# Moving the tiles of a projection kernel to other byte places, with a new order at its start and its end

## The chip, the cores and the metric

The kernel runs on one core of one Trainium2 chip. The metric is the device time of one execution in microseconds, as the median of several runs.

## What is computed

One layer of a streaming encoder, for a prompt of 4096 frames and a sample of 64 frames with a state, in float32:

```python
def mixer_layer(x, c, s_gla, s_hgrn, w_ada, b_ada, g_pre, w_in, w_alpha, b_alpha,
                g_on_gla, lb, g_on_hgrn, w_out, g_post):
    mod = jnp.einsum('bd,de->be', c, w_ada) + b_ada
    shift, scale, gate = jnp.split(mod, 3, axis=-1)
    h = rms_norm(x, g_pre) * (1 + scale[:, None]) + shift[:, None]
    p = jnp.einsum('btd,de->bte', h, w_in)               # 1024 x 3600
    q_a, k_a, v_a, z_a, a_lr, q_h, f_h, i_h, z_h = jnp.split(p, ...)
    log_alpha = log_sigmoid(a_lr @ w_alpha + b_alpha) / 16
    o_a, s_a = chunked_gla(q_a / 8, k_a, v_a, log_alpha, s_gla)      # 4 heads
    f = lb + (1.0 - lb) * sigmoid(f_h)
    o_h, s_h = chunked_gla(silu(q_h), 1.0 - f, i_h, log(f), s_hgrn)  # 4 heads
    o_a = rms_norm(o_a, g_on_gla) * silu(z_a)
    o_h = rms_norm(o_h, g_on_hgrn) * silu(z_h)
    o = jnp.concatenate([o_a, o_h], axis=-1) @ w_out     # 1024 x 1024
    return x + gate[:, None] * rms_norm(o, g_post), s_a, s_h
```

`chunked_gla` is a gated linear recurrence: the state decays by a gate in each frame and takes in key times value; the output is the query times the state.

## The kernel before

The prompt is cut into 16 groups of 256 frames; the sample's 64 frames ride along with one group in each part. The kernel has these parts, one after the other:

1. *Start* (`setup`, `first_group`). It loads x, the conditioning, the identity and eight rows of small vectors, normalises and turns the first group, computes the modulation from w_ada in eight steps of 128 features, and projects the first group in step with the arriving weights. Here the order is written out by hand.
2. *GLA part*, 16 groups (`proj_gla`). `proj_feat` (L594) computes q and k with features on the partitions, `tok_step` (L606) computes z and v with tokens on them. The recurrence of the group before (`attend`) is woven in at fixed stops.
3. *HGRN part*, 16 groups (`proj_hgrn`). f and q by `proj_feat`, i by `tok_step`; the recurrence is woven in.
4. *Last gates* (`z_tile`): z of the HGRN half by `tok_step`, tile by tile. The first stretch has the last recurrence beside it, the rest has TensorE's projections alone.
5. *Output projection* (`project`, product at L1391): 2 x 2 blocks by Strassen's scheme in Winograd's form, seven products of 12 matmuls for each group: A11 by B11, A12 by B21, S2 by T2, S3 by T3, S1 by T1, S4 by B22, A22 by T4; then norm, gate and store. The sample's rows are projected inside the last group.

Each float32 number is split into a rounded part and a rest (hi and lo), and a product has three terms: hi hi, hi lo, lo hi. A matmul has one operand that *stands* (loaded into the array, 128 columns) and one that *streams* (256 to 512 columns). The two differ between the helpers:

```python
for a, b in ((wh, hi), (wh, lo), (wl, hi)):                       # proj_feat, L593
    self.nc.tensor.matmul(ps[:, :T], a, b, ...)                   # weights stand, h streams
for i, (a, b) in enumerate(((hi, wh), (hi, wl), (lo, wh))):       # tok_step, L605
    self.nc.tensor.matmul(ps[:r, : c1 - c0], a, b, ...)           # h stands, weights stream
```

The tiles: `wa` (8 units of 4096 bytes per partition: weights of q and k, then f, then the last gates, then the blocks S1 to S4 and A22), `wv` (8 units of 4224 bytes: z, then q of HGRN, then output weights), `wb` (8 units of 4096 bytes: v, then i, then output weights), `wc` (12 units of output weights), `hh` (h split, 5 slots 5120 bytes apart), `hs` (pairs of the staging tile `wst`, used for A11 and A12). Pools are stacked from the left end of a partition's memory in the order const, small, w, then the recurrence or the output weights; x, h, e and the staging tiles are stacked from the right end. Inside a pool a tag's slots follow each other in the order of their first use.

The *place* of a tile in what follows is its byte address in its partition modulo 512. With the kernel's sizes the allocator gives:

| tile | place before |
|---|---|
| `wa`, `wb`, `wc` | 320 |
| `wv`, units in order | 320, 448, 64, 192, and again |
| `hh`, `hf`, `xt`, `e` | 224 |
| `hs` | 224 (A11) and 352 (A12) |
| `Xg`, `Qg`, `K`, `F`, `A`, `v`, `S` of the recurrence | 320 |
| `ident` | 128 |

The halves hi and lo, the steps of 128 columns and the features inside a tile are multiples of 256 or 512 bytes apart, except in `wv` while it holds z (528 columns wide), where the rest lies 64 and the second half of the columns 32 bytes further on.

TensorE executes in program order, and SP issues nearly all loads and stores in order. The planner keeps the order of most instructions on the other engines but may move some of them past each other, as in the end shown in the prediction.

Of the kernel before, what the change touches and what calls it, by code (L numbers as in the profile page):

```python
# [15 lines left out]
P = 128  # L16
D = 1024
# [11 lines left out]
class Kernel:  # L29
# [42 lines left out]
    def rstd(self, ms, n, table=False):  # L72
# [73 lines left out]
    def setup(self):  # L146
# [22 lines left out]
        nc.scalar.preload_act_table_set("natural_log_exp_and_others")  # L169
# [17 lines left out]
        with ExitStack() as s:  # L187
            one = self.pool(s, "setup")
            ap = self.pool(s, "ada", 3)

            rows = one.tile([52, P], F32, name="rows")
            v = lambda a: a.rearrange("(k p) -> k p", p=P)
            self.x_load(0, [0])
            nc.sync.dma_start(rows[0:8], v(t["c_prompt"][0]))
            nc.sync.dma_start(rows[8:16], v(t["c_sample"][0]))
            nc.sync.dma_start(self.ident, t["ident"])
            self.x_load(0, [1])
            few = [
                (rows[16:32], v(t["b_ada"][0, : 2 * D])),
                (rows[32:40], v(t["g_pre"][0])),  # L200
                (rows[40:42], v(t["b_alpha"][0])),
                (rows[42:50], t["hgrn_lb_logits"].rearrange("r (k p) -> (r k) p", p=P)),
                (rows[50:51], t["g_onorm_gla"]),
                (rows[51:52], t["g_onorm_hgrn"]),
            ]
            ada = self.ada_load(ap, 0, few[:4])
            w = self.first_load(0)
            for dst, src in few[4:]:
                nc.sync.dma_start(dst, src)
            with self.tc.manual_schedule():  # L210
                self.first_group(ap, ada, w, rows)
            for _ in self.vs0:
                pass
# [4 lines left out]
    def ada_load(self, ap, k, few=()):  # L218

        sts = []  # L220
        for i in range(2):
            st = ap.tile([P, 4, 2, P], F32, name="ada_st", bufs=10)
            for e in range(2):
                src = self.t["w_ada"][0, i * 512 : i * 512 + 512, e * D + k * P : e * D + (k + 1) * P]
                self.nc.sync.dma_start(st[:, :, e, :], src.rearrange("(n p) c -> p n c", p=P))
                for dst, src in few[2 * i + e : 2 * i + e + 1]:
                    self.nc.sync.dma_start(dst, src)
# [3 lines left out]
    def first_group(self, ap, ada, w, rows):  # L231
# [69 lines left out]
        nc.vector.tensor_copy(col[:, :16], pr[:, :16])  # L301
        self.x_norm(0, [1])
# [5 lines left out]
        )  # L308
        pts = [self.ps(n).rearrange("p (k t) -> p k t", k=2) for n in ("tp", "at", "at", "pj")]
# [8 lines left out]
        pr = self.ps("ms")  # L318
        nc.tensor.transpose(pr[:, :52], rows, self.ident[:52, :52])
# [5 lines left out]
        nc.vector.tensor_copy(col[:, 16:], pr[:, 16:52])  # L325
        nc.vector.tensor_scalar(col[:, 24:32], col[:, 24:32], 1.0, None, ALU.add)
        raw(0, nc.scalar)
        w_split(0, ws[0])
        am = ada_out(pa)
# [153 lines left out]
    def quad_norm(self, g, js):  # L483
# [3 lines left out]
        ss, half, rs = [self.small.tile([P, 8], F32, name=n) for n in ("q_ss", "q_half", "q_rs")]  # L487
# [78 lines left out]
    def split_h(self):  # L566
# [741 lines left out]
    def load_wout(self, room):  # L1308
# [7 lines left out]

        def unit():
            u = self.wunit(rooms.pop(0)[0]) if rooms else room.tile([P, 1024], F32R, name="wc", bufs=12)
            return u[:, :1024].rearrange("p (two c) -> p two c", two=2)
# [51 lines left out]
    def project(self, ogs, rest):  # L1371
# [3 lines left out]
        quarter = lambda u: u[:, :1024].rearrange("p (two k c) -> p two k c", two=2, k=4)  # L1375
        s_tile = lambda: quarter(self.wunit("wa"))
        a_tile = lambda: quarter(self.stage_pair(F32R))
# [15 lines left out]
        with ExitStack() as s:  # L1393
# [3 lines left out]
            A11, A12 = a_tile(), a_tile()  # L1397
# [68 lines left out]
            def store(ss, ys, xs, dst, last=False):  # L1466

                r = ys[0].shape[0]
                add(ss[:r, 0:1], ss[:r, 0:1], ss[:r, 1:2])
                rs = self.rstd(ss[:r, 0:1], D, table=True)  # L1470
# [46 lines left out]

            ogs = og_load(1) if ng > 1 else None
            for p in range(ng):
# [14 lines left out]

                b = self.ps("pj")
# [4 lines left out]
                if not more:  # L1540
                    sample(both, *rest_s)
                if more:
                    a11 = turn(ogs[0], "at")
                    A11 = a_tile()
                    w3, w2 = block(), block()
                    sub(w3, a11, w21)
                    sub(w2, w1, a11)
                    parts(A11, a11)
                    parts(S3, w3, nc.gpsimd)
                    parts(S1, w1, nc.gpsimd)  # L1550
                    parts(S2, w2)
# [4 lines left out]
                if more:  # L1556
                    A22, A12 = s_tile(), a_tile()
                    parts(A22, a22)
                    a12 = turn(ogs[1], "at")
                    parts(A12, a12)  # L1560
                    ogs = og_load(p + 2) if p + 2 < ng else None
# [4 lines left out]
                if more:  # L1566
                    S4 = s_tile()
                    w4 = sub(block(), a12, w2)
                    parts(S4, w4, nc.gpsimd)
# [21 lines left out]
                store(ss[1], [y21, y22], xs[2:], rows(p, 1), not more)  # L1591
                if p == ng - 2:
                    both = turn_sample(ogs)
                if more:
                    cur = dict(A11=A11, A12=A12, A22=A22, S1=S1, S2=S2, S3=S3, S4=S4)

# [46 lines left out]
    def run(self):  # L1643
# [11 lines left out]
        with ExitStack() as rec:  # L1655
# [42 lines left out]
            for g in range(ng):  # L1698
# [11 lines left out]
                h = self.split_h()  # L1710
# [93 lines left out]
```

## Time and profile before

| what | value |
|---|---|
| runs | 2062.38, 2065.14, 2065.37 us; median 2065.14 us |
| the profiled execution | 2065.15 us |
| its span, first to last instruction | 2063.4 us |
| mean granted TensorE clock | 0.995 |
| TensorE matmul, weight load busy | 99%, 87% of the span |
| VectorE, ScalarE, GpSimd busy | 73%, 53%, 15% |
| HBM | 91 GB/s over the span |

The span is what the trace covers; the time of the execution has 1.75 us more around it. PE is the matmul side of TensorE, PEld its weight loads, DVE is VectorE, ACT is ScalarE, POOL is GpSimd, SP is SyncE. A line of a group reads: line, engine, operation, written tile, read tiles, shape, count, then busy time and mean duration, then idle time of the engine just before. A line of the timeline reads: start, length, engine, line, operation, tiles, shape, count of merged instructions, and in brackets the idle time ahead with what ended it. Matmul durations overlap, and their ends are modelled.

### The profile page before, as it was taken

The numbers are of one execution on the slowest core, as the hardware profiler recorded it, in microseconds if no ns is written. First come the engines' busy times: TensorE is split into PE (matmuls) and PEld (weight loads), VectorE is DVE, ScalarE is ACT, GpSimd is POOL, SyncE is SP. The second block draws the span as 40 slices with busy tenths as digits, with TensorE's granted clock in tenths as the row PEclk, the third lists the DMA queues.
The fourth block names the chain that finished last, engine by engine and source line by source line (L and its number), as shares of the span: only waits on it lengthen the run. The fifth ranks groups of instructions, "written<-read, shape, count | busy, mean of one in ns | idle before, by whom it ended". The sixth has DMA issues, their size and how long they took to land.

```text
span 2063.4 us, 47068 instructions
## 1 busy us (share of the span) xinstructions
PE 2033.4 (99%) x17404; PEld 1796.0 (87%) x17404; DVE 1513.0 (73%) x4740; ACT 1088.9 (53%) x3207; POOL 304.1 (15%) x782
## 2 busy tenths in 40 slices
PE   8999999999999999999999999999999999999998
PEld 6888899999999888989999999999978888888886
DVE  4776777767777678777777877877786667767675
ACT  4676666777667565444444444444545544434332
POOL 0111111111111121111111111111110002333321
PEclk9999999999999999999999999999999999999999
DMA  9332222232222231011111111100246654534443
GB/s 296 97 77 64 62 58 57 64 73 62 58 56 75 82 118 44 32 37 60 52 37 51 46 65 32 38 32 32 63 139 212 216 194 149 170 131 167 140 143 103
DMA packets 236086, 190.10 MB, mean 92 GB/s; under 512 B 138208, under 2 KB 160196, under 8 KB 235856
## 3 DMA queue, kind: packets, MB, share of 16 engines
q1 hardware_dynamic: 235712, 186.83, 29.9%
q8 instruction: 137, 2.24, 0.5%
q14 instruction: 93, 0.76, 0.1%
q10 hardware_dynamic: 144, 0.26, 0.0%
HBM read 126.59 MB, written 60.43 MB: 91 GB/s over the span
## 4 chain that ended last, share of the span: by engine, by line
PE 91%; DVE 4%; ACT 3%; DMA 1%; issue 1%; POOL 0%; SPq 0%; DVEq 0%; ACTq 0%; POOLq 0%
PE ps_pj L606 32%; PE ps_pj L594 25%; PE ps_pj L1391 13%; PE ps_at L674 3%; PE ps_at L1003 2%; PE ps_ms L805 2%; PE ps_o L789 2%; PE ps_o L781 2%; PE ps_o L1391 2%; PE ps_at L910 1%; PE ps_tp L754 1%; PE ps_pj L614 1%; PE ps_at L1382 1%; PE ps_ms L781 1%; PE ps_pj L352 1%
## 5 line engine op out<-in xcount | busy, mean ns | idle before, releaser
L594 PE MATMUL ps_pj<-hh,wa 128*128 128x256 f32 (+1 forms) x2976 | 390.8, 286 | 0.6 <-ACT hh L102 0.4
L606 PE MATMUL ps_pj<-wb,hh 128*128 128x512 f32 x1536 | 386.0, 402 | 0.5 <-POOL wb L103 0.5
L594 PEld LDWEIGHTS ps_pj<-hh,wa 128*128 128x128 f32 x2976 | 369.1, 189 | 5.3 <-issue 1.7
L606 PEld LDWEIGHTS ps_pj<-wb,hh 128*128 128x128 f32 x1536 | 281.7, 189 | 66.1 <-issue 2.9
L594 PE MATMUL ps_pj<-hh,wv 128*128 128x256 f32 (+1 forms) x1536 | 196.2, 285 | 0.0
L594 PEld LDWEIGHTS ps_pj<-hh,wv 128*128 128x128 f32 x1536 | 187.4, 189 | 10.0 <-issue 9.7
L606 PE MATMUL ps_pj<-wv,hh 128*128 128x264 f32 x1464 | 191.1, 287 | 0.0
L606 PEld LDWEIGHTS ps_pj<-wv,hh 128*128 128x128 f32 x1464 | 181.5, 188 | 3.6 <-ACT e L1099 2.4
L606 PE MATMUL ps_pj<-wa,hh 128*128 128x512 f32 x768 | 182.3, 396 | 0.0
L606 PEld LDWEIGHTS ps_pj<-wa,hh 128*128 128x128 f32 x768 | 143.3, 188 | 35.0 <-issue 0.8
L1249 ACT ACTIVATE g<-ps_pj 128x256 f32<-128x256 f32 (+1 forms) x128 | 49.6, 388 | 219.3 <-PE ps_pj L594 214.3
L103 DVE TENSOR_TENSOR hh<-hf,hh 128x512 fp32r<-128x512 f32 (+1 forms) x188 | 129.9, 696 | 16.3 <-ACT hh L102 13.6
L102 ACT CAST hh<-hf 128x512 fp32r<-128x512 f32 (+1 forms) x188 | 117.2, 624 | 41.6 <-PE ps_pj L606 22.8
L816 DVE SCALAR_TENSOR_TENSOR S<-S,T,ps_ms 128x128 f32<-128x128 f32 x186 | 56.1, 340 | 81.4 <-PE ps_ms L805 81.4
L953 DVE TENSOR_TENSOR wst<-wst,T 128x160 f32<-128x160 f32 (+4 forms) x480 | 107.9, 265 | 1.4
L977 ACT ACTIVATE A<-Ac,member 128x128 f32<-128x128 f32 x256 | 80.0, 389 | 47.2 <-DVE Ac L971 47.2
L1451 ACT ACTIVATE sq<-e 128x512 bf16<-128x512 f32 x64 | 40.4, 631 | 121.0 <-DVE e L1463 121.0
L1391 PE MATMUL ps_pj<-wc,wa 128*128 128x512 f32 x384 | 98.9, 392 | 0.0
L1454 POOL TENSOR_TENSOR e<-e,gg 128x512 f32<-128x512 f32 x32 | 41.6, 1299 | 367.8 <-ACT sq L1451 367.8
L984 POOL COPY T<-T 128x16 f32<-128x16 f32 (+1 forms) x32 | 7.8, 244 | 543.7 <-DVE Qg L845 401.6
L1391 PEld LDWEIGHTS ps_pj<-wc,wa 128*128 128x128 f32 x384 | 72.0, 188 | 16.3
L971 DVE COPY_PREDICATED Ac<-mask,ps_at 128x112 f32<-128x112 uint8 (+6 forms) x448 | 82.5, 223 | 2.1 <-PE ps_at L1003 1.0
(349 smaller groups left out, 4028.2 us busy)
## 6 DMA issues: line engine op xcount, KB each, us to landing
hf<-h_d SPq DMA_DIRECT2D x128, 256.0 KB
h_d<-hf SPq DMA_DIRECT2D x64, 256.0 KB
oh_d<-e SPq DMA_DIRECT2D x64, 256.0 KB
xq<-in_x_prompt_dram SPq DMA_DIRECT2D x64, 256.0 KB
out_y_prompt_dram<-xq SPq DMA_DIRECT2D x63, 256.0 KB
xt<-in_x_prompt_dram SPq DMA_DIRECT2D x448, 32.0 KB
wst<-in_w_in_dram SPq DMA_DIRECT2D x36, 256.0 KB
e<-oh_d SPq DMA_DIRECT2D x33, 256.0 KB
```

What stands on the lines that cost most here:

```text
L102: self.nc.scalar.copy(hi, src)
L103: (eng or self.nc.vector).tensor_tensor(lo, src, hi.bitcast(F32), ALU.subtract)
L594: self.nc.tensor.matmul(ps[:, :T], a, b, start=i == 0, stop=i == n - 1)
L606: self.nc.tensor.matmul(ps[:r, : c1 - c0], a, b, start=kt == 0 and i == 0, stop=kt == KT - 1 and i == 2)
L674: nc.tensor.transpose(pt[:, i * P : (i + 1) * P], D[:, c + i, :], self.ident)
L781: mm = nc.tensor.matmul(po[h], A[:, c * 4 + h, :], v, start=h < n, stop=St is None and h == 4 - n)
L816: nc.vector.scalar_tensor_tensor(Sn[:, g, :], St[:, g, :], T[:, c * G + g, 0:1], pd[:, g, :], ALU.mult, ALU.add)
L953: nc.vector.tensor_tensor(parts(dst), parts(src), t.unsqueeze(3).to_broadcast(shape), ALU.mult)
L971: nc.vector.copy_predicated(Ach[:, :, 4 * a :].rearrange("p h (j m) -> p h j m", m=4), self.mask[:CL, : 8 - a].unsqueeze(1).unsqueeze(3).t ...
L977: nc.scalar.activation(Ah[:, :, 32 * b : 32 * b + 32], Ach, AF.Copy, scale=self.member[:CL, 8 + b : 9 + b])
L1249: nc.scalar.activation(sg, pf[:, :T], AF.Sigmoid)
L1391: nc.tensor.matmul(bank, u[:, a, kt, :], W[name][kt][:, b], start=kt + i == 0, stop=kt + i == 5)
```

## The change

It has three pieces.

*Places.* Two of the four buffers of `q_ss` and of `q_half` go (128 bytes of the pool small), an unused tile of 32 bytes stands between `wv` and `wb`, and one of 480 bytes ahead of `wc`. In the last gates, where a group has 256 frames, h begins 480 bytes further inside its slot. Among the output weights, units 2, 4, 5 and 7 of those that lie in `wv` begin 128 bytes further on, and so does A12 in its staging tile.

| tile | place after |
|---|---|
| `wa`, `wc` | 192 |
| `wb` | 224 |
| `wv`, units in order | 192, 320, 448, 64, and again; as output weights 192 or 448 |
| `hh` | 224, in the last gates 192 |
| `hs` | 224 (A11) and 480 (A12) |
| the recurrence's tiles | 224 |
| `ident`, `xt`, `e`, `hf` | as before |

*Start.* The eight rows are split into 40 (`rows`) and 12 (`later`). Four loads go to ScalarE's queue, and the preload of its table stands behind them; the identity and the second x tile come earlier on SP's queue. The first transpose takes all 40 rows, the second one of 52 rows goes, five warming matmuls stand in its place, and the other 12 rows are turned in step 1 of the eight.

*End.* The last group's seven products have an order of their own (`last`): A11 by B11, S2 by T2, the sample, S1 by T1, S4 by B22, A12 by B21, first store, S3 by T3, A22 by T4, second store. All its scalings are on VectorE. In the very last store the sum of squares of the first-known half is scaled ahead, and the other half joins it in the instruction that scales it (`rest`).

```diff
-        nc.vector.tensor_scalar(m, ms, 1.0 / n, EPS, ALU.mult, ALU.add)
+        if rest is None:
+            nc.vector.tensor_scalar(m, ms, 1.0 / n, EPS, ALU.mult, ALU.add)
+        else:
+            nc.vector.scalar_tensor_tensor(m, ms, 1.0 / n, rest, ALU.mult, ALU.add)
...
-            rows = one.tile([52, P], F32, name="rows")
+            rows, later = one.tile([40, P], F32, name="rows"), one.tile([12, P], F32, name="later")
             self.x_load(0, [0])
-            nc.sync.dma_start(rows[0:8], v(t["c_prompt"][0]))
-            nc.sync.dma_start(rows[8:16], v(t["c_sample"][0]))
             nc.sync.dma_start(self.ident, t["ident"])
             self.x_load(0, [1])
+            for dst, src in [(rows[0:8], ...), (rows[8:16], ...), (rows[16:32], ...), (rows[32:40], ...)]:
+                nc.scalar.dma_start(dst, src)
+            nc.scalar.preload_act_table_set("natural_log_exp_and_others")
...
-        nc.tensor.transpose(pr[:, :16], rows[:16], self.ident[:16, :16])
+        nc.tensor.transpose(pr[:, :40], rows, self.ident[:40, :40])
         warm(8)
...
         turn(0)
-        pr = self.ps("ms")
-        nc.tensor.transpose(pr[:, :52], rows, self.ident[:52, :52])
+        warm(5)
         turn(1)
...
+        am = ada_out(pa)
         w_split(0, ws[0])
-        am = ada_out(pa)
...
+        self.wpool.tile([P, 8], F32, name="pad", bufs=1)
...
+            if k == 1:
+                pr = self.ps("ms")
+                nc.tensor.transpose(pr[:, :12], later, self.ident[:12, :12])
+                nc.vector.tensor_copy(col[:, 40:], pr[:, :12])
...
-        ss, half, rs = [self.small.tile([P, 8], F32, name=n) for n in ("q_ss", "q_half", "q_rs")]
+        ss, half, rs = [
+            self.small.tile([P, 8], F32, name=n, bufs=b) for n, b in (("q_ss", 2), ("q_half", 2), ("q_rs", 4))
+        ]
...
-            u = self.hp.tile([P, 2, 2, T], F32R, name="hh", bufs=5)
+            if low and T == GROUP:
+                u = self.hp.tile([P, 1280], F32R, name="hh", bufs=5)[:, 120 : 120 + 4 * T]
+                u = u.rearrange("p (i j t) -> p i j t", i=2, j=2)
+            else:
+                u = self.hp.tile([P, 2, 2, T], F32R, name="hh", bufs=5)
...
+            o = 32 if tag == "wv" and i in (2, 4, 5, 7) else 0
+            return u[:, o : o + 1024].rearrange("p (two c) -> p two c", two=2)
...
-        a_tile = lambda: quarter(self.stage_pair(F32R))
+        a_tile = lambda second: quarter(self.stage_pair(F32R), 32 if second else 0)
...
+                rest = None
+                if last:
+                    rest = ss[:r, 1:2]
+                    nc.vector.tensor_scalar(rest, rest, 1.0 / D, EPS, ALU.mult, ALU.add)
+                else:
+                    add(ss[:r, 0:1], ss[:r, 0:1], ss[:r, 1:2])
+                rs = self.rstd(ss[:r, 0:1], D, table=True, rest=rest)
...
+            def last(p, cur, p1, xs, ss):
+                u2, b5 = tmp(), self.ps("o")
+                def out(q, n, u, j, a, to=None):
+                    b = self.ps("pj")
+                    product(b, cur[n], u)
+                    y = add(self.etile(), b, a)
+                    square(ss[j], q, y)
+                    to = y if to is None else to
+                    scale(to, y, q)
+                    return to
+                b = self.ps("pj")
+                product(b, cur["S2"], "T2")
+                add(u2, b, p1)
+                sample(both, *rest_s)
+                product(b5, cur["S1"], "T1")
+                u4 = add(tmp(), b5, u2)
+                y12 = out(1, "S4", "B22", 0, u4)
+                y11 = out(0, "A12", "B21", 0, p1)
+                store(ss[0], [y11, y12], xs[:2], rows(p, 0))
+                b = self.ps("pj")
+                product(b, cur["S3"], "T3")
+                u3 = add(tmp(), b, u2)
+                y22 = add(self.etile(), b5, u3)
+                square(ss[1], 1, y22)
+                scale(y22, y22, 1)
+                y21 = out(0, "A22", "T4", 1, u3, tmp())
+                store(ss[1], [y21, y22], xs[2:], rows(p, 1), True)
...
-                h = self.split_h()
+                h = self.split_h(g == ng - 1)
...
-                        hh = self.split_h()
+                        hh = self.split_h(True)
...
+            room.tile([P, 120], F32, name="pad", bufs=1)
```

More of the change, by code (lines that the diff above doesn't have):

```diff
@@ L70, in tokens, with rstd @@
         return sum(r for _, _, r, _ in tl)
-    def rstd(self, ms, n, table=False):
+    def rstd(self, ms, n, table=False, rest=None):
         nc = self.nc
@@ L225, in ada_load, with first_group @@
                 self.nc.sync.dma_start(st[:, :, e, :], src.rearrange("(n p) c -> p n c", p=P))
-                for dst, src in few[2 * i + e : 2 * i + e + 1]:
-                    self.nc.sync.dma_start(dst, src)
             sts.append(st)
         return sts
-    def first_group(self, ap, ada, w, rows):
+    def first_group(self, ap, ada, w, rows, later):
         nc, col = self.nc, self.col
@@ L308, in first_group @@
         )
+        nc.vector.tensor_scalar(col[:, 24:32], col[:, 24:32], 1.0, None, ALU.add)
+        self.x_norm(0, [1])
         pts = [self.ps(n).rearrange("p (k t) -> p k t", k=2) for n in ("tp", "at", "at", "pj")]
@@ L564, in load_hf, with split_h @@
                 self.nc.sync.dma_start(self.hf[i][:, :, GROUP:], self.h_s[:, 2 * i : 2 * i + 2, :])
-    def split_h(self):
+    def split_h(self, low=False):
         out = []
@@ L1317, in unit @@
         def unit():
-            u = self.wunit(rooms.pop(0)[0]) if rooms else room.tile([P, 1024], F32R, name="wc", bufs=12)
-            return u[:, :1024].rearrange("p (two c) -> p two c", two=2)
+            tag, i = rooms.pop(0) if rooms else ("wc", 0)
+            u = room.tile([P, 1024], F32R, name="wc", bufs=12) if tag == "wc" else self.wunit(tag)
+            o = 32 if tag == "wv" and i in (2, 4, 5, 7) else 0
+            return u[:, o : o + 1024].rearrange("p (two c) -> p two c", two=2)
         here = self.tc.keep_in_program_order
@@ L1374, in project @@
         ng = self.ng
-        quarter = lambda u: u[:, :1024].rearrange("p (two k c) -> p two k c", two=2, k=4)
+        quarter = lambda u, o=0: u[:, o : o + 1024].rearrange("p (two k c) -> p two k c", two=2, k=4)
         s_tile = lambda: quarter(self.wunit("wa"))
-        a_tile = lambda: quarter(self.stage_pair(F32R))
+        a_tile = lambda second: quarter(self.stage_pair(F32R), 32 if second else 0)
         def turn(src, tag, r=P):
@@ L1396, in project @@
             a11, a12 = [turn(o, "at") for o in ogs[:2]]
-            A11, A12 = a_tile(), a_tile()
+            A11, A12 = a_tile(False), a_tile(True)
             parts(A11, a11)
@@ L1468, in store @@
                 r = ys[0].shape[0]
-                add(ss[:r, 0:1], ss[:r, 0:1], ss[:r, 1:2])
-                rs = self.rstd(ss[:r, 0:1], D, table=True)
+                rest = None
[5 more added lines that the diff above has]
+                rs = self.rstd(ss[:r, 0:1], D, table=True, rest=rest)
                 for q in range(2):
@@ L1533, in project @@
                     add(w1, w21, a22)
+                if not more:
+                    last(p, cur, p1, xs, ss)
+                    break
                 b = self.ps("pj")
@@ L1539, in project @@
                 scale(y11, y11, 0, eng=nc.gpsimd)
[L1540 to L1551, printed above, removed]
+                a11 = turn(ogs[0], "at")
+                A11 = a_tile(False)
+                w3, w2 = block(), block()
+                sub(w3, a11, w21)
+                sub(w2, w1, a11)
+                parts(A11, a11)
+                parts(S3, w3, nc.gpsimd)
+                parts(S1, w1, nc.gpsimd)
+                parts(S2, w2)
                 b = self.ps("pj")
@@ L1555, in project @@
                 u2 = add(tmp(), b, p1)
[L1556 to L1561, printed above, removed]
+                A22, A12 = s_tile(), a_tile(True)
+                parts(A22, a22)
+                a12 = turn(ogs[1], "at")
+                parts(A12, a12)
+                ogs = og_load(p + 2) if p + 2 < ng else None
                 b = self.ps("pj")
@@ L1565, in project @@
                 u3 = add(tmp(), b, u2)
[L1566 to L1569, printed above, removed]
+                S4 = s_tile()
+                w4 = sub(block(), a12, w2)
+                parts(S4, w4, nc.gpsimd)
                 if p == ng - 2:
@@ L1590, in project @@
                 scale(y21, y21, 0)
-                store(ss[1], [y21, y22], xs[2:], rows(p, 1), not more)
+                store(ss[1], [y21, y22], xs[2:], rows(p, 1))
                 if p == ng - 2:
                     both = turn_sample(ogs)
-                if more:
-                    cur = dict(A11=A11, A12=A12, A22=A22, S1=S1, S2=S2, S3=S3, S4=S4)
+                cur = dict(A11=A11, A12=A12, A22=A22, S1=S1, S2=S2, S3=S3, S4=S4)
     def og_half(self, p, j, q, ap=None):
```

29 lines of the change are left out of this document (14 added, 15 removed).

## The prediction

> **What bounds the kernel now.** I read the page first, then the groups by shape, then short stretches of the timeline on TensorE, because one row already says which engine counts.
>
> ```profile
> span 2063.4 us, 47068 instructions
> PE 2033.4 (99%) x17404; PEld 1796.0 (87%) x17404; DVE 1513.0 (73%) x4740; ACT 1088.9 (53%) x3207; POOL 304.1 (15%) x782
> PE 91%; DVE 4%; ACT 3%; DMA 1%; issue 1%; POOL 0%; SPq 0%; DVEq 0%; ACTq 0%; POOLq 0%
> ```
>
> TensorE is busy 99% of the span and makes up 91% of the chain that ended last. So the spacing of the matmuls is the time, and what the change does to that spacing is the question. The groups that it touches most:
>
> ```profile
> L606 PE MATMUL ps_pj<-wb,hh 128*128 128x512 f32 x1536 | 386.0, 402 | 0.5 <-POOL wb L103 0.5
> L594 PE MATMUL ps_pj<-hh,wa 128*128 128x256 f32 x2784 | 360.8, 284 | 0.6 <-ACT hh L102 0.4 <-DVE hh L103 0.2
> L606 PE MATMUL ps_pj<-wa,hh 128*128 128x512 f32 x768 | 182.3, 396 | 0.0
> L594 PE MATMUL ps_pj<-hh,wv 128*128 128x256 f32 x1440 | 181.5, 283 | 0.0
> ```
>
> Behind the arrow stand the two operands of a matmul: in L606 rows the weights (wb, wa, wv) stream and h (hh) stands, in L594 rows h streams and the weights stand. The mean in ns is one matmul from its start to its modelled end, which overlaps the next; the spacing has to come from runs without interruption (start, length, count):
>
> ```profile
> 762.35 3.31 PE L594 MATMUL ps_pj<-hh,wv 128*128 128x256 f32 x27
> 1462.80 3.92 PE L594 MATMUL ps_pj<-hh,wa 128*128 128x256 f32 x32
> 119.60 3.48 PE L594 MATMUL ps_pj<-hh,wa 128*128 128x256 f32 x28
> 944.16 7.16 PE L606 MATMUL ps_pj<-wb,hh 128*128 128x512 f32 x30
> 1561.82 138.29 PE L606 MATMUL ps_pj<-wa,hh 128*128 128x512 f32 x592
> ```
>
> Length less one matmul, over count less one: h on wv (3.31 - 0.28)/26 = 116.5 ns; h on wa (3.92 - 0.28)/31 = 117.4 ns in the HGRN part and (3.48 - 0.28)/27 = 118.5 ns in the GLA part; wb on h (7.16 - 0.40)/29 = 233.1 ns; wa on h (138.29 - 0.39)/591 = 233.3 ns. The shapes and the order of the three terms are the same wherever the widths are the same, yet the spacing differs. What differs is the tiles' places (byte address modulo 512, table above). The rows of the output projection show the lower end:
>
> ```profile
> 2020.74 1.53 PE L1391 MATMUL ps_pj<-wc,wa 128*128 128x512 f32 x6
> 2022.11 0.84 PE L1391 MATMUL ps_pj<-wv,wa 128*128 128x512 f32 x3
> 2022.79 0.84 PE L1391 MATMUL ps_pj<-wb,wa 128*128 128x512 f32 x3
> 2023.47 1.52 PE L1391 MATMUL ps_pj<-wc,wa 128*128 128x512 f32 x6
> ...
> 2027.07 0.86 PE L1391 MATMUL ps_pj<-wb,hs 128*128 128x512 f32 x3
> 2027.77 0.86 PE L1391 MATMUL ps_pj<-wc,hs 128*128 128x512 f32 x3
> ```
>
> From 2022.11 the product A22*T4 runs with a standing tile at 320 and streams at 64, 320, 320: distances 256, 0, 0. Start to start it is 0.68 us for three, 226.7 ns each. The row before it, also at distance 0 but in a product that began at another distance, needs 1.37/6 = 228.3: a disturbed phase takes some matmuls to settle. A11*B11 at 2027.07 (standing 224, streaming 320, distance 96) needs 0.70/3 = 233.3. So distance 0 or 256 is worth 6.6 ns of 233 for a 512 wide matmul. For 256 wide ones wv itself holds the comparison, since its units are 4224 bytes long and step through 320, 448, 64, 192. Two neighbouring units, h at 224:
>
> ```profile
> L594 PE MATMUL ps_pj<-hh,wv x3: 277/278/278, 762.9 to 763.2; 128*128 128x256 f32 x3
> L594 PE MATMUL ps_pj<-hh,wv x3: 280/280/282, 763.3 to 763.5; 128*128 128x256 f32 x3
> ```
>
> The first stands at 192 (h is 32 above it), the second at 64 (160 above). Their matmuls differ by 3 ns at least. Over the run the two kinds alternate at a mean of 116.5, so I split it into 115.0 and 118.0. The second is what wa has now (h 416 above it, the same modulo 256), and its runs at 117.4 and 118.5 fit.
>
> **The change part by part.** *h streaming on wa*, 32 above instead of 416: 1344 matmuls of the GLA part from 118.5 to 115.0 save 4.7 us, 1440 of the HGRN part from 117.4 to 115.0 save 3.5; the 192 that are 320 wide about 0.1. That is 8.3 us. Bounds: nothing, if a constant 32 settles at the slow unit's 118.0 (0.7 less 0.9 us); 12.8 us if it reaches half of 226.7, 113.35. I take the fast unit, since it is measured at that very distance. *h on wv*: the four places rotate by 128, so the same distances come in another order: 0. *wb streaming on h*, 96 to 0: 1536 matmuls. They come in short runs between other work and start disturbed, so I take 228.5, near the row at 228.3, and not 226.7: 4.6 x 1536 = 7.1 us. Upper bound 6.4 x 1536 = 9.8. The lower bound is a row where tiles at distance 0 were not clean:
>
> ```profile
> 6.54 1.78 PE L294 MATMUL ps_pj<-zero 128*128 128x512 f32 x7
> 8.38 0.60 PE L313 MATMUL ps_at<-ident,xt 128*128 128x128 f32 x4
> 8.81 0.38 PE L313 MATMUL ps_pj<-ident,xt 128*128 128x128 f32 x2
> ```
>
> The warming matmuls stream and stand from one tile, distance 0, and need (1.78 - 0.39)/6 = 231.7 ns. That leaves 1.4 x 1536 = 2.2 us. *wa streaming on h in the last gates*, h moved by 480 bytes to 192, distance 0: 720 matmuls (the group with the sample keeps its layout, 48) run on end for 138 us and have time to settle, so 227.0: 6.3 x 720 = 4.5 us, bounds 1.2 (at 231.7) and 4.8. *Output projection*: wv units that were 128 or 384 from wa come to 0 or 256; wc stays at 0; wb goes from 0 to 32, and A11 and A12 change from 96 and 480 to 480, with wb at 0. Better: S2, S3, S4 starts and two units of A11, A12; worse: wb in the products that are clean now. Between 233 and 227 for a part of 1344 matmuls I take 1.5 us, bounds -1 and 3.
>
> *The recurrence's tiles* move from 320 to 224 against the identity at 128 and the staging tiles. The L313 rows are a streaming identity at 128 against xt at 224: 0.43/4 = 108 ns, with nothing to see of a conflict. Cost 0, kept as a rival. *Fewer buffers for q_ss and q_half*: two calls of quad_norm at most are in flight, two are enough, 0; were they not, ScalarE would wait, which is 53% busy.
>
> *The start.* Four of the eight small loads go to ScalarE's queue ahead of its table load; the other four are no longer needed before the first group.
>
> ```profile
> 12.50 0.32 PE L319 MATMUL ps_ms<-ident,rows 52*128 52x52 f32 x1 [3.31 <-DMA rows<-in_g_onorm_hgrn_dram]
> 5.00:10.00 5.00, 3.12 (x17) 2.49 (x17) 1.74 (x8) 2.28 (x8) 0.00 (x0) 1.00 0.87 251
> 10.00:15.00 5.00, 2.50 (x13) 1.96 (x17) 2.14 (x9) 0.98 (x2) 0.00 (x0) 0.67 0.93 276
> 20.00:25.00 5.00, 5.00 (x42) 3.82 (x41) 3.97 (x10) 3.04 (x8) 0.00 (x0) 0.81 1.14 318
> ACT wa L102 <- DMA e<-in_w_in_dram: 3.2, 5, 1.1
> ```
>
> TensorE's 3.31 us wait goes; late next is the second x tile, some 1.5 us before 12.50, and the five added warming matmuls (5 x 0.23 = 1.2 us) fall in that wait and keep the granted clock (0.67 in 10 to 15 us) up. But the eight steps after it stream weights at a DMA share of 1.1, and ScalarE already waits 3.2 us for them, so the gain is capped by how much earlier the stream fills: shares 0.87 and 0.93 against 1.14 in 10 us are about (0.27 + 0.21)/1.14 x 5 = 2.1 us. I take 2.0, bounds 0 and 4. The table load moves behind four issues on ScalarE; it has until the first x tile lands, so 0; without that cover it would cost one issue each. The transpose of 12 rows moved to step 1 is one short matmul and a DVE copy under TensorE's work: 0.3 us at most. SP loses four issues ahead of the weights.
>
> *The end.*
>
> ```profile
> 2052.86 1.52 PE L1391 MATMUL ps_pj<-wc,wa 128*128 128x512 f32 x6
> 2054.42 0.69 DVE L1463 TENSOR_TENSOR e<-ps_pj,tmp 128x512 f32<-128x512 f32 x1 [0.23 <-PE ps_pj L1391]
> 2055.67 1.42 DVE L1472 SCALAR_TENSOR_TENSOR xq<-e,nwt_y,xq 128x512 f32<-128x512 f32 x2
> 2057.00 0.69 DVE L1454 TENSOR_TENSOR e<-e,gg 128x512 f32<-128x512 f32 x1
> 2059.03 1.41 DVE L1472 SCALAR_TENSOR_TENSOR xq<-e,nwt_y,xq 128x512 f32<-128x512 f32 x2
> 2060.47 0.38 ACTq L1473 DMA_DIRECT2D out_y_prompt_dram<-xq  x1
> ```
>
> After the last matmul (2054.38) DVE adds, then finishes the other half's store (2055.67 to 2057.09) before it scales. The new order has that store two products earlier, so the scale follows the add and 2 us of DVE leave the tail; two scalings that move from POOL to DVE (0.69 each) and a one-column step lie under the last two products, tightly. I take 1.5, bounds 1 and 2.
>
> Sum: 8.3 + 7.1 + 4.5 + 1.5 + 2.0 + 1.5 = 24.9 us. Where matmuls alternate with the recurrence, a faster TensorE meets DVE a little sooner (the chain's 9% off TensorE): of the 15.4 us there I give back 10%, 1.5. Left are 23.4 us. The profiled execution took 2065.15 us, its span 2063.4 and 1.75 around it, and stands 0.01 above the median of 2065.14. So 2041.7, which I put at **2042**.
>
> **The rivals.** *Places do nothing*: the differences would come from what else runs. Then only start and end count, 2065.15 - 3.5 = 2061.6. Against it: 226.7 and 233.3 in one product group, and the two neighbouring units of wv, 0.4 us apart. The Trainium skill, TensorE: Matmul & The Clock Gate, section "Step-by-step: what each phase is for", states this rule: TensorE reads its streaming and its standing operand through two independent ports, by which a tile's place could not matter and the sum would be the 3.5 us of this rival. The trace does not agree, by the same 226.7 and 233.3. *Distance 0 stays disturbed*: the gains of wb and the last gates shrink to their lower bounds of 2.2 and 1.2, 8.2 us less, 2050. For it: the warming row; against it: 2022.11. *DVE takes over*: half of the 15.4 us comes back as waits, about 6 more, 2048.
>
> ```profile
> 1100.00:1300.00 200.00, 200.00 (x1990) 183.64 (x1989) 156.50 (x534) 92.47 (x256) 25.98 (x91) 1.00 0.13 42
> L674 PE MATMUL ps_at<-ident,A 128*128 128x128 f32 x480 | 71.6, 275 | 0.0
> L1003 PE MATMUL ps_at<-wst,K 128*32 128x128 f32 x1024 | 35.4, 276 | 0.7 <-DVE wst L953 0.7
> ```
>
> DVE is 78% busy in that stretch, so there is room. *Slower*: the recurrence's small matmuls run into conflicts because their tiles move by 96 bytes while the identity and the staging tiles stay. The L674 and L1003 groups are 107 us; over 23.4/107 = 22% on them takes the gain away, and at 30% (32 us) it is 2074. For it: they meet a distance that no run of theirs had. Against it: the L313 rows.
>
> **How the numbers follow.** Forecast 0.66 with its own range 2032 to 2049; distance 0 disturbed 0.15; DVE 0.10; places do nothing 0.06; slower 0.03. The range 2029 to 2054 goes down to the upper bounds of the terms (36 us together) and up past the second and third. 0.2%, or 4 us, is about what a measurement of this kernel can tell from no change: faster 0.91, the same 0.06 (places do nothing: 2061.6 is 0.17%), slower 0.03.
>
> **What would show it.** Runs of h on wa at 115 ns; wb on h mostly under 229; the last gates' long run at 227 instead of 233.3; A22*T4 not far above 226.7; no 3.3 us wait at the start and a DMA share over 1 sooner; under 7.5 us from the last matmul to the end instead of 9.0. Runs at 118 and 233 again would make the prediction wrong, as would TensorE waits on DVE that grow by as much.

## The result, and the profile after

The changed kernel takes 2053.44 us (median; 2051.72 to 2053.86) against 2065.14 us, a ratio of 0.9948 with the interval 0.9934 to 0.9961. It is faster by 11.7 us, half of the 23.4 that were forecast. The profiled execution of it took 2052.96 us. The page of the changed kernel:

```profile
span 2051.1 us, 47070 instructions
PE 2020.9 (99%) x17409; PEld 1791.1 (87%) x17409; DVE 1514.6 (74%) x4742; ACT 1088.4 (53%) x3207; POOL 302.4 (15%) x780
PE 88%; DVE 4%; ACT 4%; DMA 2%; SPq 1%; issue 1%; POOL 0%; DVEq 0%; ACTq 0%; POOLq 0%
```

TensorE is still busy 99% of the span, and its share of the chain is 88% instead of 91%: no other engine has taken over, so I look for the missing 11.7 us in the spacing of its matmuls and at the two ends. The groups by shape, after:

```profile
L620 PE MATMUL ps_pj<-wb,hh 128*128 128x512 f32 x1536 | 380.2, 399 | 0.5 <-POOL wb L106 0.5
L608 PE MATMUL ps_pj<-hh,wa 128*128 128x256 f32 x2784 | 357.5, 283 | 0.6 <-ACT hh L105 0.4 <-DVE hh L106 0.2
L608 PE MATMUL ps_pj<-hh,wv 128*128 128x256 f32 x1440 | 180.5, 282 | 0.0
L620 PE MATMUL ps_pj<-wa,hh 128*128 128x512 f32 x768 | 178.0, 391 | 0.0
```

wb on h lost 5.8 us of busy time, wa on h 4.3, h on wa only 3.3. The sharpest view for this is the chain: it cuts the program into pieces (start, length, engine, written tile, line, count), and a piece ends where the next one starts, so length by count is the spacing, with no modelled end in it (the entry of the piece is counted in). Pieces of before, one of each kind:

```profile
422.02 5.79 PE ps_pj L606 x24
427.81 4.27 PE ps_pj L594 x36
434.15 2.85 PE ps_pj L594 x24
808.26 6.90 PE ps_pj L594 x59
1560.58 140.00 PE ps_pj L606 x600
1723.59 8.28 PE ps_pj L1391 x36
```

and the same pieces after:

```profile
419.44 5.67 PE ps_pj L620 x24
425.11 4.20 PE ps_pj L608 x36
431.38 2.81 PE ps_pj L608 x24
434.63 2.84 PE ps_pj L608 x24
802.80 6.92 PE ps_pj L608 x59
1552.66 136.01 PE ps_pj L620 x600
1711.56 8.32 PE ps_pj L1409 x36
```

The last gates go from 233.3 to 226.7 ns (140.00/600 and 136.01/600). A piece of 24 with wb on h saves 0.12 us. A run of 36 with h on wa goes from 118.6 to 116.7 ns, not to 115.0, and the runs of 24 behind it to 117.1 and 118.3. The 59 products with h on wv and a piece of the output projection are a little longer than before.

### The profile page after: what moved, and what is told of

Its sections match the earlier page's. It is cut to its first block, busy times and chain, and to the rows that moved or that the text cites. A ratio compares the mean times of both kernels' runs of the same rounds, so it can differ in the third digit from the quotient of the medians.

```text
span 2051.1 us, 47070 instructions
## 1 busy us (share of the span) xinstructions
PE 2020.9 (99%) x17409; PEld 1791.1 (87%) x17409; DVE 1514.6 (74%) x4742; ACT 1088.4 (53%) x3207; POOL 302.4 (15%) x780
## 4 chain that ended last, share of the span: by engine, by line
PE 88%; DVE 4%; ACT 4%; DMA 2%; SPq 1%; issue 1%; POOL 0%; DVEq 0%; ACTq 0%; POOLq 0%
PE ps_pj L620 31%; PE ps_pj L608 24%; PE ps_pj L1409 13%; PE ps_at L688 3%; PE ps_at L1017 2%; PE ps_ms L819 2%; PE ps_o L803 2%; PE ps_o L1409 2%; PE ps_o L795 2%; DMA wst<-in_w_in_dram 1%; PE ps_at L924 1%; PE ps_tp L768 1%; PE ps_pj L628 1%; ACT A L991 1%; ACT A L936 1%; PE ps_at L1400 1%
## 5 line engine op out<-in xcount | busy, mean ns | idle before, releaser
L620 PE MATMUL ps_pj<-wb,hh 128*128 128x512 f32 x1536 | 380.2, 399 | 0.5 <-POOL wb L106 0.5
L620 PE MATMUL ps_pj<-wa,hh 128*128 128x512 f32 x768 | 178.0, 391 | 0.0
L1469 ACT ACTIVATE sq<-e 128x512 bf16<-128x512 f32 x64 | 40.4, 632 | 119.5 <-DVE e L1481 117.1
L1472 POOL TENSOR_TENSOR e<-e,gg 128x512 f32<-128x512 f32 x30 | 38.9, 1296 | 337.6 <-ACT sq L1469 337.6
```

What stands on the lines that cost most here:

```text
L620: self.nc.tensor.matmul(ps[:r, : c1 - c0], a, b, start=kt == 0 and i == 0, stop=kt == KT - 1 and i == 2)
```

## The experiments

"Place" is the byte address modulo 512 throughout; "distance" is the place of the streaming operand less that of the standing one. Times of runs are medians, but each of the two sweeps is a single execution; ratios are to the kernel before. In code, `...` stands for lines that are not shown.

**Start and end alone.** All places as before.

```diff
-        self.wpool.tile([P, 8], F32, name="pad", bufs=1)
...
-        ... bufs=b) for n, b in (("q_ss", 2), ("q_half", 2), ("q_rs", 4))
+        ss, half, rs = [self.small.tile([P, 8], F32, name=n) for n in ("q_ss", "q_half", "q_rs")]
...
-            o = 32 if tag == "wv" and i in (2, 4, 5, 7) else 0
+            o = 0
...
-                h = self.split_h(g == ng - 1)
+                h = self.split_h()
...
-            room.tile([P, 120], F32, name="pad", bufs=1)
```

> The new order at the start and at the end alone, every tile at its place of before. The ledger of the two profiles gives 0.65 us for the start (first wb matmul at 55.35 instead of 56.00) and 1.0 us for the end (8.35 instead of 9.37 us after the last output matmul begins), so theory 1 (the places carry the rest) expects 2063.5 us. The rival, that places do little and the new orders carry the gain, expects under 2058.

2063.35 us, ratio 0.9991 (0.9982 to 1.0). The two orders are worth 1.8 us, which is at the edge of what the interval can tell from nothing; the places are worth the other 10, so the places act.

**All operands at 224.** wa, wb, wc and h are at distance 0, in the last gates too.

```diff
+        self.wpool.tile([P, 8], F32, name="pad", bufs=1)        # ahead of wa
...
-        self.wpool.tile([P, 8], F32, name="pad", bufs=1)        # between wv and wb
...
-                h = self.split_h(g == ng - 1)
+                h = self.split_h()
...
-            room.tile([P, 120], F32, name="pad", bufs=1)
```

> The changed kernel with every weight tile, wa and wc too, at h's place 224, so that all projections and products stream and stand at distance 0 modulo 256 (q of HGRN at 0 and 128 in turn). Theory 1: 0 is the one clean distance at both widths, 32 is not; h on wa falls from 117.0 to about 113.5 to 114.5 ns, the output products from 231 to 228; 2784 x 3 ns and 1344 x 3 ns are 12 us, less some waits: 2043 us. Theory 2: standing weights want h 32 above them; h on wa rises to 118 or more, only the output projection gains 4 us: 2052.

2053.91 us, ratio 0.9946 (0.9933 to 0.9958): the first theory, with 2043, fell, and the second, with 2052, came nearer. In the chain of this kernel a run with h on wa is longer than before and after the change, the output projection shorter:

```profile
426.09 4.31 PE ps_pj L607 x36
804.93 7.02 PE ps_pj L607 x59
1717.27 8.16 PE ps_pj L1408 x36
```

4.31/36 = 119.7 ns. So the distance that is best for a 512 wide product is bad for a 256 wide one.

**The same, with q of HGRN also at distance 0 or 256.**

```diff
+        if tag == "wv" and w == 512:
+            o = 32 * (self.wv_odd % 2)
+            self.wv_odd += 1
```

> As the one before, and every second unit of wv begins 128 bytes later while it holds q of HGRN, so that h on wv is at distance 0 too. Theory 1: 1440 matmuls from 117.2 to 114 ns, 4 to 5 us less than the one before: 2039 us. Theory 2 (h should be 32 above): no less than the one before, 2052 or more.

2054.63 us, ratio 0.9946 (0.9933 to 0.996). The products on wv went to 119.9 ns as well (mean inside runs; 118.9 in the kernel above, 117.0 before the change), so here too 0 is no clean distance for a 256 wide product.

**wa and wb at 256.** h on wa at 480, wb on h at 32, wa on h at 64. From the kernel with all at 224, with the two removed lines on h and wc put back:

```diff
-        self.wpool.tile([P, 8], F32, name="pad", bufs=1)
+        self.wpool.tile([P, 16], F32, name="pad", bufs=1)
```

> A point of the sweep: wa and wb at 256, so h on wa has distance -32 (224), wb on h 32, wa on h in the last gates 64, wc on wa 224. Theory 1 (distance 0 alone is clean): h on wa 117 to 119 ns, wb on h 231 to 235, the last gates 231 to 235; 2066 us. A rule by which any small distance is good gives 228 for wb on h and 2053.

2063.72 us, ratio 0.999 (0.998 to 1.0). Mean inside runs: h on wa 118.25, wb on h 233.2, as before the change; wa on h 229.2. 32 helps only in one direction, and 64 is half good for a 512 wide product.

**A sweep of the distance.** Every group's h lies 32 bytes further on than the last one's.

```diff
+        self.h_places = [32 * (i % 16) for i in range(1, 64)]
...
-            if low and T == GROUP:
-                u = self.hp.tile([P, 1280], F32R, name="hh", bufs=5)[:, 120 : 120 + 4 * T]
+            if T == GROUP:
+                if i == 0:
+                    at = self.gate_places.pop(0) if low else self.h_places.pop(0)
+                u = self.hp.tile([P, 1280], F32R, name="hh", bufs=5)[:, at // 4 : at // 4 + 4 * T]
```

> The changed kernel, with each group's h at its own place: after each splitting of a prompt group's h, 32 bytes further on (modulo 512), so that the feature products (256 wide, h streaming, weights 32 bytes below h's first place) and the token products (512 wide, weights streaming over h) run at all sixteen distances in one execution, once in the first recurrence and once in the second; the last gates run at distances 0, 256, 64, 128, 32, 192, 96 and so on. Theory 1, a table with a narrow good place for each width: token products 227 ns at 0 and 256 and 231 to 236 at the rest, feature products near 116.6 to 117 at 32 bytes (and perhaps at 288) and 118 to 120 at the rest; 2057 us in all. Theory 2, only the equal place counts for token products and nothing but noise lies between the distances of the feature products (117 to 119.9 in no order, unequal in the two recurrences); 2057 us too, told apart by the table alone.

2060.68 us, 3.7 more than both theories had. Mean spacing in ns, with the distance modulo 256, since d and d + 256 gave the same within 2 ns, mostly within 0.5 (wb on h and h on wa; stalled products and the unsettled beginnings of runs left out, with which the 512 wide products at 0 come to 228.7 and 228.9; the second line of each width is the later sweep below, with wa at 32):

| distance | 0 | 32 | 64 | 96 | 128 | 160 | 192 | 224 |
|---|---|---|---|---|---|---|---|---|
| 512 wide, first sweep | 227.9 | 233.5 | 228.8 | 233.5 | 233.0 | 234.2 | 233.3 | 233.3 |
| 512 wide, second | 227.6 | 233.3 | 228.9 | 233.4 | 233.3 | 234.3 | 233.5 | 233.4 |
| 256 wide, first sweep | 119.8 | 116.8 | 116.3 | 120.0 | 118.9 | 118.3 | 114.5 | 118.2 |
| 256 wide, second | 119.9 | 117.1 | 117.8 | 120.0 | 118.8 | 117.9 | 113.5 | 118.4 |

Neither theory had this. The two recurrences repeat each other, so it is no noise; the 512 wide products have a second good place at 64, and the 256 wide ones have their best at 192, not at 32, and their worst at 0 and 96.

**Output weights in matching units.** The products on A11 and A12 (places 224 and 480) get the wb units at 224, those on S and A22 (192) the units at 192 and 448.

```diff
+            if n in ("B11", "B21"):
+                return self.wunit("wb")[:, :1024].rearrange("p (two c) -> p two c", two=2)
```

> The changed kernel, with the output weights laid out so that the two products on the A tiles (place 224) stream from the units at 224 and the five on the S tiles (place 192) stream from those at 192, so that every output product runs at distance 0 modulo 256. Theory 1, the output projection lost its gain to products at 32 bytes and they spoil their neighbours: its stage falls from 344.9 us to the 340.6 that it took with everything at 224, and the time to 2049. It is also the kernel with all at 224 but for the feature products at 32 instead of 0, so 4 to 5 us below that kernel's 2053.9 prices these. Theory 2, the feature products at 32 are worth nothing in all, since what they gain waits at the ends of their runs: 2052 to 2054.

2050.72 us, ratio 0.9926 (0.9912 to 0.9939): 2.7 us less than the change, 3.2 less than the kernel with all at 224. A piece of 36 of the projection in the chain, and a row of the timeline with the products on A11 and A12:

```profile
1711.71 8.24 PE ps_pj L1411 x36
...
2032.87 2.92 PE L1411 MATMUL ps_pj<-wb,hs 128*128 128x512 f32 x12
```

The piece took 8.32 us in the changed kernel and 8.16 with all at 224. So the products that streamed from another distance than 0 (wb at 32 from wa, wv and wc at 224 from A11 and A12) were a loss, and a part of what was expected came back. The twelve products on A12 keep (2.92 - 0.39)/11 = 230 ns at distance 0 modulo 256; why is not settled.

**wb back at 96.** From the changed kernel; wc stays at 192.

```diff
-        self.wpool.tile([P, 8], F32, name="pad", bufs=1)
+        self.wpool.tile([P, 32], F32, name="pad", bufs=1)
...
-            room.tile([P, 120], F32, name="pad", bufs=1)
+            room.tile([P, 96], F32, name="pad", bufs=1)
```

> The changed kernel, with the streaming weights of the token products back at 96 bytes above h (the standing weights stay 32 below h, the last gates at 0). Theory 1, the token products' spacing counts: 1320 of them go from 229.2 to 233.4 ns, 5.5 us, less some 1 us that waits at the ends of runs: 2058. Theory 2, other engines fill their stage: 2054.

2058.31 us, ratio 0.9968 (0.9955 to 0.998): 4.9 us above the change, as the first theory had it. Not all of it is the token products' own: between the two profiles the products with wb on h, counted from each start to the next start in the two recurrences, take 371.3 us instead of 367.4, and the output projection, whose weights lie in the same tiles, takes 1.2 us longer.

**The standing weights alone.** The same, and h in the last gates at 224 again.

```diff
-                h = self.split_h(g == ng - 1)
+                h = self.split_h()
...
-                        hh = self.split_h(True)
+                        hh = self.split_h()
```

> The part of the change that puts the standing weights 32 bytes below h, alone with the new start and end (token products at 96, last gates at a disturbed 480). Against the new start and end alone (2063.35). Theory 1, the spacing inside runs counts whole: 2580 products by 1.3 ns, 3.4 us less: 2060. Theory 2, what the runs gain is waited for at their ends (these waits grew by 3.2 us between the two kernels), so the part is worth 1 us or less: 2062.5 to 2063.5.

2063.0 us, ratio 0.999 (0.9981 to 0.9999), only 0.35 below start and end alone. The number fits the second theory, but its reason does not hold. Between the profiles of these two kernels the products with h on wa in the two recurrences, counted from each start to the next start, take 339.8 us instead of 342.1, 2.3 us less, and the output projection (from its first matmul on wc) takes 1.9 us longer (344.2 to 346.1), because the output weights lie in the same tiles. The clock distorts the comparison further. Windows of this kernel, of the changed one and of start and end alone (us, busy time and count of PE, PEld, DVE, ACT and POOL, granted clock, DMA share, GB/s):

```profile
71.00:76.00 5.00, 4.77 (x26) 4.57 (x27) 3.54 (x8) 3.88 (x10) 0.00 (x0) 0.66 0.23 82
```

```profile
71.00:76.00 5.00, 4.78 (x39) 4.57 (x40) 4.15 (x9) 4.34 (x11) 0.00 (x0) 1.00 0.34 126
```

```profile
767.00:772.00 5.00, 4.84 (x55) 4.49 (x55) 2.66 (x17) 1.12 (x3) 0.63 (x3) 0.66 0.37 101
```

A mean of 0.66 over five microseconds is a clock of one half over 3.4 us, and costs up to 0.34 x 5 = 1.7 us: in the first window TensorE began 26 products, in the second, at full clock, 39. In this kernel the slow stretch falls mostly on products with h on wa, so their gain of 2.3 us is understated. In start and end alone it falls into the HGRN part, so up to 1.7 of the 1.9 us by which that part is shorter here (751.0 to 749.2 us) may be clock, not spacing. Each of the two profiles has one such stretch between the first token product and the last gates, so their totals may be compared. Spacing did pay, and the median shows what it cost in the output projection.

**The standing weights 192 below h.** From the kernel with matching units; five small constants move from the front of the memory to between wv and wb, so that wa comes to 32, while wb and h stay at 224.

```diff
+        self.wpool.tile([P, 8], F32, name="pad0", bufs=1)
...
-        self.mask = c.tile([P, NMASK], U8, name="mask")        # and member, half, lb, oml
+        self.mask = w.tile([P, NMASK], U8, name="mask", bufs=1) # after wv, ahead of wb
...
-        ...[:, 120 : 120 + 4 * T]
+        ...[:, 16 : 16 + 4 * T]
```

> The kernel with the output weights in their matching units (2050.72), and the standing weights of the feature products moved from 32 to 192 bytes below h, the distance at which the sweep spaced these products at 114.5 ns; the streaming weights, the last gates and all output products stay at 0 modulo 256. Theory 1, spacing counts wherever the engine is not waiting: 2580 products from 117.0 to 114.5 ns (6.4 us) and 1340 of the second recurrence from 117.2 to some 115.5 (2.3 us), 8.7 us in all: 2042. Theory 2, as between the start and end alone and the standing part alone, what the feature products gain comes back as waits at the ends of their runs: 2049 to 2051. Between them, 2044 to 2047, a part comes back.

2044.5 us, ratio 0.9907 (0.989 to 0.9923): 6.2 us less, of 8.7 expected by the first theory; the waits did not take it back. Where the rest is, the chain shows:

```profile
422.17 4.24 PE ps_pj L609 x36
428.44 2.83 PE ps_pj L609 x24
431.71 2.74 PE ps_pj L609 x24
800.85 6.70 PE ps_pj L609 x59
```

The products on wv fell to 113.6 ns (6.70/59). But of the three runs on wa, at one and the same distance, two are at 117.8 and 117.9 ns and the third at 114.2 with its entry, 113.3 inside. Of the 85 longer runs (17 products or more) 37 keep 113 and 46 keep 118 to their end.

**The sweep again, wa at 32.** The edit of the first sweep, on the last kernel; h in the last gates stays at 288.

> The last kernel (standing weights at 32, streaming weights at 224), with each group's h at its own place, 32 bytes further each time, as in the first sweep, where the standing weights were at 192. Theory 1, the distance alone counts: the feature products give the first sweep's table by distance (119.8 ns at 0, 116.6 at 32, 116 to 118 at 64, 120 at 96, 118.7 at 128, 118 at 160, 114.5 at 192, 118.2 at 224), and the 115.9 at 192 in the last kernel is of h's own place. Theory 2, the place of h alone counts, or that of the weights: the low value stays at h's place 128 or 384 (distance 96 here), or the table is another. Time near 2052 either way.

2055.89 us, 4 more than expected. The table above: by distance the two sweeps agree within 1.5 ns, so for the 256 wide products the distance counts, not either place. For wb on h the second sweep is only a repeat, since neither moved; but the last gates of the first sweep, with wa (192) streaming instead of wb (224), give 227.0 at 0, 229.1 at 64 and 234.2 at 160, so the distance counts there too. And a group whose h lay 448 above wa (192 modulo 256), the token products before it at a disturbed distance, had all its runs at the low value:

```profile
384.27 4.10 PE ps_pj L612 x36
388.81 1.39 PE ps_pj L612 x12
390.41 2.75 PE ps_pj L612 x24
```

In the first sweep it was not so: there a group at 192, with the token products before it at a disturbed distance (128), had a run at 2.83/24 = 117.9 ns beside one at 114.6. So a disturbed distance of the token products does not settle the matter alone:

```profile
259.02 2.83 PE ps_pj L612 x24
262.29 2.75 PE ps_pj L612 x24
```

**wb 64 above h.** From the kernel with wa at 32.

```diff
+        w.tile([P, 16], F32, name="pad", bufs=1)      # ahead of wb: 288
...
-            if n in ("B11", "B21"):  # wb
+            if n in ("B11", "B21"):  # eight units of wc at 480, the last four of the others at 32
```

> The kernel with the standing weights 192 bytes below h (2044.5), with the streaming weights of the token products moved from h's place to 64 bytes above it (229.0 ns in the sweeps where 0 had 227.3), and the output weights divided so that the products stay at 0 modulo 256. In the kernel at 192 each run of feature products keeps one of two spacings from its first few products on, 117.8 ns after token products at 0 and 113.3 in the sweeps after token products at other distances. Theory 1, how the run is entered sets it: most runs at 113.3, 1500 products by 4.5 ns less, 6.7 us, against some 1 to 2 us at the token products: 2039 to 2041. Theory 2, the entry has nothing to do with the token products' place: the two spacings stay, 2045 to 2047.

2040.69 us, ratio 0.9877 (0.9861 to 0.9894). It is the fastest version: 12.75 us below the change, 25 below the kernel before. The same three runs:

```profile
422.10 4.11 PE ps_pj L610 x36
428.25 2.76 PE ps_pj L610 x24
431.44 2.74 PE ps_pj L610 x24
```

76 of the 85 runs now keep 113 ns, and the mean inside runs on wa went from 115.9 to 114.35, 4.0 us over 2580 products, beside a measured 3.8. The token products, every run at 228.9 once settled, cost hardly more than at distance 0 with their unsettled beginnings (means 229.6 and 229.4). So how a run is entered decides between its two spacings, and the forecast held. But the edit does not show that the token products do it. The recurrence's tiles lie behind wb and move by 64 bytes with it, and many of the runs follow two, four or eight transposes of a tile of the recurrence, A, and not a token product. Of the 46 runs at 118 in the kernel that this one was made from, 23 came right behind token products and 22 behind two or eight transposes; here 4 and 3 are left. Which of the two moves did it, and what keeps seven runs at 118, is open.

## Why the prediction was wrong, and what of it held

By parts, the 12.3 us between the two spans are 0.65 at the start, 4.1 in the GLA part (from the first token product to the first with h on wv), 3.1 in the HGRN part (to the first of the last gates; of which up to 1.7 may be the clock: the profile of before has a stretch of 3.4 us at half clock there, at 769 us, the changed one none), 4.3 in the last gates, -0.8 in the output projection and 0.9 at the end. The forecast had 2.0, 13.9 for the two recurrences together, 4.5, 1.5 and 1.5.

*h streaming on wa* (8.3 us): this step failed. Its mechanism, a spacing that goes with the places, is what the runs show; its size is not. The prediction split a mean of 116.5 into 115.0 and 118.0 by two neighbouring units of wv and said: "I take the fast unit, since it is measured at that very distance". What it had measured there was the lengths of the matmuls, whose ends are modelled. The starts in the trace do lie 114.7 and 118.7 ns apart in these two units, but they are three products each in a row that alternates between two distances modulo 256, and no run of theirs was long enough to settle. In a run of its own, 32 gives 116.7 (4.20/36). The mean inside runs went from 118.3 to 117.0, so the term is 2580 x 1.3 = 3.4 us; counted from each start to the next, with the entries of the runs, it is 2.5 (342.0 to 339.4 us). In that mean 25 of 85 runs still stand at 118; in the kernel with wb back at 96, where the recurrence's tiles lie elsewhere too, there are 3. The 115 and the 8 us exist, but at 192: the last two kernels took 10 us there, wv included. The upper bound, 113.35 as half of 226.7, was the right number at the wrong place, by luck.

*wb on h* (7.1): 4.9, counted from each start to the next (372.3 to 367.4 us; each profile has one stretch at half clock among these products). The kernel with wb at 96 gives 3.9 for the same products, and up to 1.2 more, since the changed kernel's hold 2.4 us at half clock and that kernel's none. The spacing inside runs went from 233.4 to 229.2, 0.7 short of the 228.5 assumed, and 1320 products lie inside runs, not 1536: 5.5 us.

*wa on h in the last gates* (4.5): right. 140.00 less 136.01 is 4.0 for 600 products, and 4.7 us lie between the kernels with the last gates at 480 and at 0.

*Output projection* (1.5): wrong in sign. Its stage took 344.9 us after 344.1. I had counted clean and disturbed products apart; a disturbed one also spoils the clean ones behind it. Timeline rows after (length one matmul over the spacing times count less one):

```profile
2005.16 0.84 PE L1409 MATMUL ps_o<-wv,wa 128*128 128x512 f32 x3
2005.84 0.86 PE L1409 MATMUL ps_o<-wb,wa 128*128 128x512 f32 x3
2006.54 1.55 PE L1409 MATMUL ps_o<-wc,wa 128*128 128x512 f32 x6
2007.93 0.84 PE L1409 MATMUL ps_pj<-wv,wa 128*128 128x512 f32 x3
```

Start to start, wv at 0 needs 0.68/3 = 226.7, wb at 32 0.70/3 = 233.3, and wc, at distance 0, still 1.39/6 = 231.7. With every product at 0 modulo 256, in the kernel with matching units, 2.7 us of time came back.

*Start* (2.0): TensorE's first projection matmul came 2.5 us earlier, the first token product only 0.65 (56.00 to 55.35). The cap was named and set too high. Windows and a wait of the changed kernel:

```profile
5.00:10.00 5.00, 3.54 (x10) 2.78 (x11) 2.38 (x13) 2.69 (x8) 0.00 (x0) 1.00 1.04 303
10.00:15.00 5.00, 4.51 (x42) 3.42 (x41) 0.82 (x2) 1.35 (x3) 0.00 (x0) 1.00 0.77 215
ACT wa L105 <- DMA e<-in_w_in_dram: 11.3, 6, 2.7
```

The DMA share rose to 1.04 in the first window and fell to 0.77 in the second, 1.81 after 1.80 in sum: by 15 us no more had come than before, and ScalarE's wait for weights grew from 3.2 to 11.3 us.

*End* (1.5): about 1.0. From the end of the last matmul 8.0 us are left where 7.5 were expected:

```profile
2041.56 1.54 PE L1409 MATMUL ps_pj<-wc,wa 128*128 128x512 f32 x6
2042.09 1.41 DVE L1496 SCALAR_TENSOR_TENSOR xq<-e,nwt_y,xq 128x512 f32<-128x512 f32 x2
2043.42 0.68 DVE L1472 TENSOR_TENSOR e<-e,gg 128x512 f32<-128x512 f32 x1
2044.02 0.68 DVE L1481 TENSOR_TENSOR e<-ps_pj,tmp 128x512 f32<-128x512 f32 x1
```

The last matmul is done at 2043.10, but VectorE finishes the first store at 2043.50 and then scales the other block (L1472), and the add that needs the last product starts at 2044.02. "So the scale follows the add" held; the add was late.

*Waits* (1.5 given back): right in size, though a tenth was only assumed. Inside runs 3.4 and 5.5 us were gained, 8.9 together, and counted from start to start 2.5 and 4.9, 7.4 together; so about 1.5 us went at the ends of runs. No new engine shows: VectorE is at 74% after 73%.

The rivals: *places do nothing* fell with start and end alone. *Distance 0 stays disturbed* held for 256 wide products, not for the 512 wide ones that it was said of. *DVE takes over* did not happen. *Slower* did not either: four transposes of the recurrence (`ps_at`) take 0.44 us in the chain before and after, and the GLA and HGRN parts without their four large groups of projections (h on wa, h on wv, wb on h, wv on h) take 374.4 us before and 375.1 after.

## What to carry to other kernels

Where TensorE is busy all the time, as here, sweep the byte distance between streaming and standing operand in one run (give each group its own offset) before choosing it; each width has its own good distance, and a tile that serves two widths should have its place settled for both. Read a spacing from long pieces of the chain, never from three products, and count the neighbours too: a product at a bad distance slows the good ones behind it, and how a run is entered can fix its pace. A kernel that undoes one part moves everything that shares its tiles, so read its stages before its total, and look first in which stage each profile has its slow stretches of the clock.

## What the hardware showed unexpectedly

The spacing of the matmuls in this kernel depends on the distance of the two operands modulo 256 bytes: 226.7 to 234 ns at 512 wide, 113.3 to 120 at 256 wide. At 192 a 256 wide run has two stable paces, 113.3 and 117.8, and keeps to its end the one that it has after its first few products. The Trainium skill, TensorE: Matmul & The Clock Gate, section "Step-by-step: what each phase is for", has two independent read ports, by which loading weights takes nothing from the running matmul, and a gap of some 216 ns at 512. No long run here came below 226.7, and the gap moved with the place; the measurement decides.

The clock can drop to half for 3.4 us in the middle of the kernel. Twelve of the thirteen profiles have one or two such stretches between the first token product and the last gates, at about 72, 191 or 767 us, where TensorE's work is broken by short waits; edits elsewhere move them from one of these spots to another. In the kernel with the standing weights alone TensorE was busy 2.31 of the 3.40 us before. What sets them off is not shown.
